# The second score matmul of each head on 64 array rows instead of 128, the two heads of a pair on different rows

## The chip, the cores and the metric

The kernel runs on one core of a Trainium2 chip. The metric is device time in microseconds of one execution, lower is better. The kernel before has a median of 1741.18 us over three runs (1739.69 to 1743.17).

## What is computed

One layer of a diffusion backbone over 1024 latent and 128 context tokens, in fp32 with D_MODEL 1024: a modulated RMSNorm, one input projection, a Fourier mixer beside windowed attention, gates, an output projection, and an MLP with 4096 hidden units. The change lies in the attention: 16 query heads in 4 groups that share a key and value head, head size 64, blocks of 128 queries. In the reference:

```python
scores = jnp.einsum('btkgd,blkd->bkgtl', qb, k_all,
                    preferred_element_type=jnp.float32) * (HEAD_DIM ** -0.5)
if mask is not None:
    scores = jnp.where(mask[None, None, None], scores, NEG_INF)
sink_col = ...
p = jax.nn.softmax(jnp.concatenate([scores, sink_col], axis=-1), axis=-1)[..., :-1]
return jnp.einsum('bkgtl,blkd->btkgd', p.astype(v_all.dtype), v_all)
```

A latent block sees up to 384 latent keys around it and the 128 cached ones (512 keys, 384 at the two ends); the context block sees 128 keys.

## The kernel before

**Two halves of a number.** TensorE (PE) multiplies in a rounded fp32 type. To keep fp32 accuracy a value is split into hi (rounded) and lo (the rest, `sub`, L138), and a product is made as hi·hi + hi·lo + lo·hi (`mm3`, L191 to L193). The scores use the short head size to do this in two matmuls instead of three. `qhl` holds, for each of four heads, 64 columns of q hi and then 64 columns of q lo; transposed (L670) and copied (L675) it is `qT`, with q hi in array rows 0 to 63 and q lo in rows 64 to 127. The keys lie twice, one copy above the other: `kth` has k hi in both halves, `ktl` has k lo in both. The first matmul (L691, `qT` with `kth`) gives q hi·k hi + q lo·k hi, the second (L692, `qT` with `ktl`) adds q hi·k lo + q lo·k lo, into the same PSUM tile `s`, of which there are two.

**Staging.** A unit is a group of four heads and a block of 128 queries: 4 groups by 9 blocks are 36 units. For each, `attention_q` projects q (24 matmuls of 256 columns, L191 to L193), rotates it on VectorE (DVE, `apply_rope`), splits and transposes it; `attention_scores` makes the scores pair by pair (two heads e = 0, 1 in each of two pairs): two matmuls a head, then on DVE the mask and the row maximum (L693), on ScalarE (ACT) the exponential (L705), on GpSimd (POOL) the division (L715). `attention_out` transposes the probabilities (L729), splits them (ACT L734, DVE L138) and multiplies with v (L739, L740) into `o`. There are 144 matmuls of L691 and 144 of L692: of each 96 with 512 columns, 32 with 384 and 16 with 128. Between the units stand gate projections (`mm`, 24 matmuls of 384 columns each), put there to fill PE.

**What sets the order.** The order on each engine is chosen by a scheduler when the kernel is built, from the dependences, the buffers and its own estimate of times. Each engine then runs its instructions in that fixed order, and waits where an operand or a buffer isn't ready. So the places of the score matmuls among the others can differ from the order in the source.

**Matmuls on fewer than 128 rows.** The kernel has few. Where the modulation is folded (`make_h`, L437) 14 small fp32 matmuls multiply 4 rows with 2 columns, and two multiply 2 rows; the built program gives these 32 of the array's rows, and shows them twice each in the trace, since fp32 takes two passes. Another fp32 matmul, L265, folds on all 128 rows and gives 16 columns.

Of the kernel before, what the change touches and what calls it, by code (L numbers as in the profile page):

```python
# [10 lines left out]
F32 = mybir.dt.float32  # L11
# [3 lines left out]
ALU = mybir.AluOpType  # L15
# [3 lines left out]
P = 128  # L19
# [38 lines left out]
def backbone_kernel(  # L58
# [25 lines left out]
    nc = tc.nc  # L84
    uid = [0]

    def nm(s):
        uid[0] += 1
        return f"{s}_{uid[0]}"
# [47 lines left out]
    def sub(eng, dst, raw, hi):  # L137
        eng.tensor_tensor(dst, raw, hi.bitcast(F32), ALU.subtract)  # L138
# [51 lines left out]
    def mm3(out, ah, al, bh, bl, start, stop):  # L190
        nc.tensor.matmul(out, ah, bh, start=start, stop=False)  # L191
        nc.tensor.matmul(out, ah, bl, start=False, stop=False)  # L192
        return nc.tensor.matmul(out, al, bh, start=False, stop=stop).ins  # L193
# [133 lines left out]
    with ExitStack() as sf:  # L327
# [169 lines left out]
        for o in range(0, NDFT, 1024):  # L497
            n = min(1024, NDFT - o)
# [8 lines left out]
        for gi in range(4):  # L507
# [17 lines left out]
            for s in range(4):  # L525
                r = slice(s * 512, (s + 1) * 512)
                anchor = mm3(pa, sth[:, s], stl[:, s], dhi[:, r], dlo[:, r], s == 0, s == 3)
            for s in range(2):
                r = slice(2048 + s * 256, 2304 + s * 256)
# [39 lines left out]
    with ExitStack() as s1x:  # L569
# [15 lines left out]
        def apply_rope(dst, src, t, hi=None):  # L585
            a = p1.tile([P, 4, HD], F32, tag="ra", name=nm("ra"), bufs=2)
            b = p1.tile([P, 4, HD], F32, tag="rb", name=nm("rb"), bufs=1)
            nc.vector.tensor_tensor(a, src, rope[:, 0, t, :].unsqueeze(1).to_broadcast([P, 4, HD]), ALU.mult)
            sw = src.rearrange("p h (d two) -> p h d two", two=2)
            sn = rope[:, 1, t, :].unsqueeze(1).to_broadcast([P, 4, HD])  # L590
            nc.vector.tensor_tensor(
                b.rearrange("p h (d two) -> p h d two", two=2),
                sw[:, :, :, ::-1],
                sn.rearrange("p h (d two) -> p h d two", two=2),
                ALU.mult,
            )
            nc.vector.tensor_tensor(dst, a, b, ALU.add)
            if hi is not None:
                nc.vector.tensor_tensor(hi, a, b, ALU.add)

        def put_v(src, t):
            vv = p1.tile([P, NG, 2, HD], F32R, tag="qhl", name=nm("qhl"), bufs=2)
# [35 lines left out]
        q1 = s1x.enter_context(tc.tile_pool(name="q1", bufs=1, space=PSUM))  # L638
# [14 lines left out]
        def attention_q(g, i, qw):  # L653
            psq = q1.tile([P, 512], F32, tag="q", name=nm("q"), bufs=1)
            r = slice(i * P, (i + 1) * P)
            for k in range(KC):
                wh, wl = qw[k // 4]
                mm3(psq[:, :256], h_hi[k][:, r], h_lo[k][:, r], wh[:, k % 4, :], wl[:, k % 4, :], k == 0, k == KC - 1)
            qsrc = psq[:, :256].rearrange("p (h d) -> p h d", h=4)
            qr = p1.tile([P, 4, HD], F32, tag="qr", name=nm("qr"), bufs=2)  # L660
            qhl = p1.tile([P, 4, 2, HD], F32R, tag="qhl", name=nm("qhl"), bufs=2)
            if i < 8:
                apply_rope(qr, qsrc, i, qhl[:, :, 0, :])
            else:
                nc.scalar.copy(qr, qsrc)
                nc.scalar.copy(qhl[:, :, 0, :], qsrc)
            sub(nc.vector, qhl[:, :, 1, :], qr, qhl[:, :, 0, :])
            psT = q1.tile([P, 512], F32R, tag="ptp", name=nm("ptp"), bufs=2)
            for h in range(4):
                ins = nc.tensor.transpose(  # L670
                    psT[:, h * P : (h + 1) * P], qhl[:, h].rearrange("p a d -> p (a d)"), identr
                )
            anchor = ins.ins
            qT = p1.tile([P, 4, P], F32R, tag="qT", name=nm("qT"), bufs=2)
            nc.scalar.copy(qT.rearrange("p h t -> p (h t)"), psT)  # L675
            return qT, anchor

        def attention_scores(g, i, qT):
            k0, nb = KWIN[i]
            n = nb * P  # L680
            m0 = MWIN[i] * P
            pts = []
            for pr in range(2):
                pt = p1.tile([P, 2, 516], F32, tag="pt", name=nm("pt"), bufs=4)
                mx = p1.tile([P, 8], F32, tag="mx", name=nm("mx"), bufs=4)
                h0 = g * 4 + pr * 2
                nc.gpsimd.tensor_copy(pt[:, :, n : n + 1], sink8[:, h0 : h0 + 2].unsqueeze(2))
                for e in range(2):
                    h = pr * 2 + e
                    sp = q1.tile([P, 512], F32, tag="s", name=nm("s"), bufs=2)  # L690
                    nc.tensor.matmul(sp[:, :n], qT[:, h, :], kth[:, k0 * P : k0 * P + n], start=True, stop=False)  # L691
                    nc.tensor.matmul(sp[:, :n], qT[:, h, :], ktl[:, k0 * P : k0 * P + n], start=False, stop=True)  # L692
                    nc.vector.tensor_tensor_reduce(  # L693
                        out=pt[:, e, :n],
                        in0=sp[:, :n],
                        in1=mask[:, m0 : m0 + n],
                        scale=1.0,
                        scalar=sink8[:, h0 + e : h0 + e + 1],
                        op0=ALU.add,
                        op1=ALU.max,  # L700
                        accum_out=mx[:, e : e + 1],
                    )
                nc.vector.tensor_scalar(mx[:, 2:4], mx[:, 0:2], -0.125, None, ALU.mult)  # L703
                for e in range(2):
                    nc.scalar.activation(  # L705
                        pt[:, e, : n + 1],
                        pt[:, e, : n + 1],
                        AF.Exp,
                        bias=mx[:, 2 + e : 3 + e],
                        scale=0.125,  # L710
                        accum_out=mx[:, 4 + e : 5 + e],
                    )
                nc.vector.reciprocal(mx[:, 6:8], mx[:, 4:6])  # L713
                for e in range(2):
                    nc.gpsimd.tensor_scalar(pt[:, e, :n], pt[:, e, :n], mx[:, 6 + e : 7 + e], 1.0, ALU.mult, ALU.mult)  # L715
                pts.append(pt)
            return pts
# [31 lines left out]
        kth = p1.tile([P, 12 * P], F32R, name="kth")  # L749
        ktl = p1.tile([P, 12 * P], F32R, name="ktl")  # L750
# [53 lines left out]
        for q in range(3):  # L804
            put_k(kv[0][0], q)
        nxt = attention_q(0, 0, qw)
        pending = None
        for s, (g, i) in enumerate(units):
            qT, anchor = nxt
            if s + 1 < len(units):  # L810
                g1, i1 = units[s + 1]
                if i1 == 0:
                    qw = load_q(g1)
                nxt = attention_q(g1, i1, qw)
                anchor = nxt[1]
            pts = attention_scores(g, i, qT)
            if i == 0 and g:
                put_k(kv[g][0], 2)
            if g + 1 < NG:
                if i == 2:  # L820
                    kv[g + 1] = load_kv(g + 1)
                if i == 4:
                    put_k(kv[g + 1][0], 0)
                if i == 7:
                    put_k(kv[g + 1][0], 1)
            if pending is not None:
                attention_out(*pending)
                if s % SKIP:
                    filler(1, anchor)
                if s <= 30:  # L830
                    mod_step(MOD_A)
            pending = (g, i, pts, kv[g][1])
            if s >= len(units) - 2:
                if s == len(units) - 2:
                    filler(100, anchor)
                    load_fx()
                f_unit(NF)
# [34 lines left out]
    with ExitStack() as sao:  # L872
# [11 lines left out]
        for m in range(KC):  # L884
            if m < 7:
                hi, lo = ER[:, 2 * m * NT : (2 * m + 1) * NT], ER[:, (2 * m + 1) * NT : (2 * m + 2) * NT]
            else:
                hi, lo = (p3.tile([P, NT], F32R, name=nm("at7")) for _ in range(2))
            for j in range(NJ):
                r = slice(j * CH, (j + 1) * CH)  # L890
# [930 lines left out]
```

## Time and profile before

| | us |
|---|---|
| median of three runs | 1741.18 |
| the profiled execution | 1740.25 |
| its span, first to last instruction | 1738.5 |
| attention stage (the units), from the span's start | about 276 to 722 |
| PE busy over the span | 1660.2 (95%) |
| DVE, ACT, POOL busy | 1217.1, 846.3, 229.2 |

Times in the trace are from the span's start. PE is TensorE's matmuls, PEld its weight loads (LDWEIGHTS), which run beside the matmul before. A matmul's row gives its start and a duration with the time it spends in the array's pipeline, so matmuls overlap: what one costs in a stream is the distance from its start to the next start. "128\*128 128x512" is array rows by columns, then the shape of what it writes or reads. "x4" stands for four that follow each other. The mean granted TensorE clock is 0.982 of full speed.

### The profile page before, as it was taken

To read this page: it belongs to the slowest core of one execution; us is meant where nothing else is said; L and a number is where in the kernel's file an instruction comes from. 1 tells how busy PE (TensorE), PEld (TensorE's weight loads), DVE (VectorE), ACT (ScalarE), POOL (GpSimd) and SP (SyncE) were. 2 spreads that over 40 slices of the span, in tenths; PEclk is the share of its full clock that TensorE was granted. 3 is DMA by queue.
4 is the path that set the end of the run, shared out by engine and by line. 5 is a ranking of instruction groups with operands and counts; after the bars stand their busy time and mean duration, and the time that the engine had idled before them with its cause. 6 is when DMAs were issued, how large, how long until landed. Compare 5 with 4: busy or idle time off the path is not lost.

```text
span 1738.5 us, 26472 instructions
## 1 busy us (share of the span) xinstructions
PE 1660.2 (95%) x9101; PEld 1480.9 (85%) x9101; DVE 1217.1 (70%) x2538; ACT 846.3 (49%) x1676; POOL 229.2 (13%) x310
## 2 busy tenths in 40 slices
PE   6999988999999999999899889999999999999998
PEld 5788878999899999999888688888888788888886
DVE  7595455686767777659968878767666488777764
ACT  7443134555646556655326663444444345444542
POOL 3410002212213222202211400000000100000000
PEclk9999999999999999999999989999999999999999
DMA  9462383032222211478655435444444997566751
GB/s 293 124 189 82 129 233 76 28 96 68 60 53 63 59 35 40 147 241 281 211 165 204 160 103 176 164 146 164 151 146 155 231 378 252 190 193 193 238 176 61
DMA packets 218759, 267.44 MB, mean 154 GB/s; under 512 B 30768, under 2 KB 150144, under 8 KB 218624
## 3 DMA queue, kind: packets, MB, share of 16 engines
q1 hardware_dynamic: 210368, 255.79, 46.3%
q0 software_dynamic: 8256, 9.96, 2.2%
q8 instruction: 72, 1.18, 0.3%
q14 instruction: 63, 0.52, 0.1%
HBM read 196.20 MB, written 69.48 MB: 153 GB/s over the span
## 4 chain that ended last, share of the span: by engine, by line
PE 43%; DVE 4%; DMA 2%; ACT 1%; issue 1%; POOL 0%; SPq 0%; ACTq 0%; DVEq 0%; POOLq 0%
PE x L1570 6%; PE x L1569 6%; PE x L1568 6%; PE x L1179 5%; PE x L1181 5%; PE x L1180 5%; PE x L1015 1%; PE x L1016 1%; PE x L1017 1%; DVE macc L302 1%; PE mm L1570 1%; PE mm L1569 1%; PE mm L1568 1%; PE mm L1226 1%; PE mm L1225 1%
## 5 line engine op out<-in xcount | busy, mean ns | idle before, releaser
L138 DVE TENSOR_TENSOR wlo<-wraw,whi 128x1024 fp32r<-128x1024 f32 x100 | 125.8, 1260 | 58.1 <-ACT whi L143 57.7
L143 ACT CAST whi<-wraw 128x1024 fp32r<-128x1024 f32 x98 | 102.5, 1049 | 88.8 <-DMA wraw<-in_w_ff_dram 21.0
L1569 PE MATMUL x<-BR 128*128 128x512 f32 x336 | 131.4, 391 | 0.0
L1570 PE MATMUL x<-BR 128*128 128x512 f32 x336 | 130.9, 391 | 0.0
L1568 PE MATMUL x<-BR 128*128 128x512 f32 x336 | 129.9, 391 | 0.0
L715 POOL TENSOR_SCALAR pt<-pt,mx 128x512 f32<-128x512 f32 (+2 forms) x144 | 99.1, 701 | 211.1 <-DVE mx L713 198.1
L705 ACT ACTIVATE pt<-pt,mx 128x513 f32<-128x513 f32 (+2 forms) x144 | 94.8, 661 | 55.8 <-DVE mx L703 55.1
L192 PE MATMUL mm<-BR,whi 128*128 128x384 f32 x336 | 113.8, 339 | 0.0
L693 DVE CUSTOM_DVE_ANT_0 pt<-s,mask,sink 128x512 f32<-128x512 f32 (+2 forms) x144 | 94.2, 673 | 22.2 <-PE ptp L729 15.0
L191 PE MATMUL mm<-BR,whi 128*128 128x384 f32 x304 | 105.3, 346 | 0.0
L193 PE MATMUL mm<-BR,wlo 128*128 128x384 f32 x304 | 102.9, 339 | 0.0
L1541 ACT CAST BR<-aa 128x512 fp32r<-128x512 f32 x80 | 49.7, 621 | 103.9 <-PE x L1569 49.1
L138 DVE TENSOR_TENSOR pl<-ptp,ph 128x512 fp32r<-128x512 f32 (+1 forms) x136 | 85.9, 640 | 15.6 <-ACT ph L734 14.5
L734 ACT CAST ph<-ptp 128x512 fp32r<-128x512 f32 (+1 forms) x136 | 72.7, 548 | 40.8 <-PE ptp L729 39.2
L302 DVE SCALAR_TENSOR_TENSOR macc<-mraw,siluc,macc 128x256 f32<-128x256 f32 x168 | 85.1, 544 | 10.5 <-DMA mraw<-in_w_ada_dram 10.3
L1179 PE MATMUL x<-BR,whi 128*128 128x512 f32 (+2 forms) x204 | 82.3, 403 | 6.2 <-ACT ZR L1203 3.3
L1181 PE MATMUL x<-BR,wlo 128*128 128x512 f32 (+2 forms) x204 | 81.1, 398 | 3.5 <-DVE wlo L138 3.5
L1180 PE MATMUL x<-BR,whi 128*128 128x512 f32 (+2 forms) x204 | 80.5, 395 | 0.0
L729 PE MATMUL ptp<-ident,pt 128*128 128x128 f32 x496 | 75.1, 273 | 3.0 <-ACT qT L675 3.0
L138 DVE TENSOR_TENSOR BR<-aa,BR 128x512 fp32r<-128x512 f32 x80 | 55.2, 689 | 32.0 <-ACT BR L1541 31.6
L1568 PEld LDWEIGHTS x<-BR 128*128 128x128 f32 x336 | 63.5, 189 | 13.2
L1569 PEld LDWEIGHTS x<-BR 128*128 128x128 f32 x336 | 63.4, 189 | 13.3
(422 smaller groups left out, 5119.6 us busy)
## 6 DMA issues: line engine op xcount, KB each, us to landing
aa<-hr_d SPq DMA_DIRECT2D x108, 256.0 KB, 3.4
ab<-in_w_ff_dram SPq DMA_DIRECT2D x108, 256.0 KB, 3.4
hr_d<-ZR SPq DMA_DIRECT2D x104, 256.0 KB, 4.1
wraw<-in_w_in_dram SPq DMA_DIRECT2D x40, 512.0 KB, 4.1
wraw<-in_w_ff_dram SPq DMA_DIRECT2D x34, 512.0 KB, 3.8
mraw<-in_w_ada_dram SPq DMA_DIRECT2D x96, 128.0 KB, 3.1
wraw<-in_w_out_dram SPq DMA_DIRECT2D x24, 512.0 KB, 3.8
z_d<-z SPq DMA_DIRECT2D x48, 192.0 KB, 1.9
```

Of the source, the lines that this page charges most:

```text
L138: eng.tensor_tensor(dst, raw, hi.bitcast(F32), ALU.subtract)
L143: nc.scalar.copy(hi, raw)
L191: nc.tensor.matmul(out, ah, bh, start=start, stop=False)
L192: nc.tensor.matmul(out, ah, bl, start=False, stop=False)
L193: return nc.tensor.matmul(out, al, bh, start=False, stop=stop).ins
L302: nc.vector.scalar_tensor_tensor(acc[:, tok, :], wa, sc_, acc[:, tok, :], ALU.mult, ALU.add)
L1179: nc.tensor.matmul(po, wh, xh, start=(k == 0 and not cont), stop=False, skip_group_check=cont)
L1180: nc.tensor.matmul(po, wh, xl, start=False, stop=False, skip_group_check=cont)
L1181: nc.tensor.matmul(po, wl, xh, start=False, stop=(k == 3), skip_group_check=cont)
L1568: nc.tensor.matmul(ps, xh, bh, start=start, stop=False, skip_group_check=cont)
L1569: nc.tensor.matmul(ps, xh, bl, start=False, stop=False, skip_group_check=cont)
L1570: nc.tensor.matmul(ps, xl, bh, start=False, stop=stop, skip_group_check=cont)
```

## The change

The second matmul of each head now runs on 64 array rows. For head e = 0 of a pair these are rows 0 to 63, for e = 1 rows 64 to 127. So that q hi lies in those rows, the odd heads have hi and lo exchanged in `qhl` (`q_hi` takes the places 0 and 3 of a pair's four, `q_lo` the places 1 and 2). The first matmul is not touched: it sums both halves, in either order. The second gives q hi·k lo alone; the term q lo·k lo is no longer computed. Both PSUM tiles of a pair are taken before the first of its matmuls, and in the source the four matmuls of a pair now stand as first, first, second, second, with the two 64-row ones side by side.

```diff
@@ apply_rope
             nc.vector.tensor_tensor(dst, a, b, ALU.add)
             if hi is not None:
-                nc.vector.tensor_tensor(hi, a, b, ALU.add)
+                a2, b2 = (x.rearrange("p (r e) d -> p r e d", r=2) for x in (a, b))
+                nc.vector.tensor_tensor(hi, a2, b2, ALU.add)
@@ attention_q
             qhl = p1.tile([P, 4, 2, HD], F32R, tag="qhl", name=nm("qhl"), bufs=2)
+            q4 = qhl.rearrange("p (r e) a d -> p r (e a) d", r=2)
+            q_hi, q_lo = q4[:, :, 0:4:3, :], q4[:, :, 1:3, :]
             if i < 8:
-                apply_rope(qr, qsrc, i, qhl[:, :, 0, :])
+                apply_rope(qr, qsrc, i, q_hi)
             else:
                 nc.scalar.copy(qr, qsrc)
-                nc.scalar.copy(qhl[:, :, 0, :], qsrc)
-            sub(nc.vector, qhl[:, :, 1, :], qr, qhl[:, :, 0, :])
+                nc.scalar.copy(q_hi, qsrc.rearrange("p (r e) d -> p r e d", r=2))
+            sub(nc.vector, q_lo, qr.rearrange("p (r e) d -> p r e d", r=2), q_hi)
@@ attention_scores
+                sps = [q1.tile([P, 512], F32, tag="s", name=nm("s"), bufs=2) for _ in range(2)]
+                kr_ = slice(k0 * P, k0 * P + n)
                 for e in range(2):
-                    h = pr * 2 + e
-                    sp = q1.tile([P, 512], F32, tag="s", name=nm("s"), bufs=2)
-                    nc.tensor.matmul(sp[:, :n], qT[:, h, :], kth[:, k0 * P : k0 * P + n], start=True, stop=False)
-                    nc.tensor.matmul(sp[:, :n], qT[:, h, :], ktl[:, k0 * P : k0 * P + n], start=False, stop=True)
+                    nc.tensor.matmul(sps[e][:, :n], qT[:, pr * 2 + e, :], kth[:, kr_], start=True, stop=False)
+                for e in range(2):
+                    half_ = slice(64 * e, 64 * e + 64)
+                    nc.tensor.matmul(sps[e][:, :n], qT[half_, pr * 2 + e, :], ktl[half_, kr_], start=False, stop=True)
+                for e in range(2):
+                    sp = sps[e]
                     nc.vector.tensor_tensor_reduce(
```

In the changed kernel the first matmul is L694, the second L697; the other lines of the attention move down by 3 to 7. The number of matmuls is the same (9061 in the built program). Since the scheduler sets the order, the pairs have to be looked for in the built program. PE's rows for the two pairs of one unit of the first group follow; `s` with its number is one head's scores, `o` the product with v, `q` a later unit's projection, `ptp` a transpose. The first pair, before:

```order
L729 MATMUL ptp_4848<-ident,pt_4631 128x128 x4
L691 MATMUL s_4963<-kth,qT_4811 128x512
L692 MATMUL s_4963<-ktl,qT_4811 128x512
L691 MATMUL s_4967<-kth,qT_4811 128x512
L692 MATMUL s_4967<-ktl,qT_4811 128x512
L739 MATMUL o_4706<-ph_4712,vg_2724 128x256
```

and in the changed program:

```order
L736 MATMUL ptp_4848<-ident,pt_4631 128x128 x4
L694 MATMUL s_4963<-kth,qT_4811 128x512
L694 MATMUL s_4964<-kth,qT_4811 128x512
L697 MATMUL s_4963<-ktl,qT_4811 128x512
L697 MATMUL s_4964<-ktl,qT_4811 128x512
L746 MATMUL o_4706<-ph_4712,vg_2724 128x256
```

The two first matmuls stand together now, and the two on 64 rows (L697) are neighbours, with a 128-row matmul ahead and one behind. The second pair of the same unit stands so on PE before:

```order
L193 MATMUL q_5296<-qwh_5292,BR 128x256
L691 MATMUL s_4980<-kth,qT_4811 128x512
L692 MATMUL s_4980<-ktl,qT_4811 128x512
L739 MATMUL o_4847<-ph_4853,vg_2724 128x256
L740 MATMUL o_4847<-pl_4854,vg_2724 128x256
L739 MATMUL o_4847<-ph_4853,vg_2724 128x256
L740 MATMUL o_4847<-pl_4854,vg_2724 128x256
L739 MATMUL o_4847<-ph_4866,vg_2724 128x256
L691 MATMUL s_4984<-kth,qT_4811 128x512
L692 MATMUL s_4984<-ktl,qT_4811 128x512
L740 MATMUL o_4847<-pl_4867,vg_2724 128x256
```

and in the changed program:

```order
L193 MATMUL q_5296<-qwh_5292,BR 128x256
L694 MATMUL s_4980<-kth,qT_4811 128x512
L697 MATMUL s_4980<-ktl,qT_4811 128x512
L746 MATMUL o_4847<-ph_4853,vg_2724 128x256
L747 MATMUL o_4847<-pl_4854,vg_2724 128x256
L746 MATMUL o_4847<-ph_4853,vg_2724 128x256
L747 MATMUL o_4847<-pl_4854,vg_2724 128x256
L746 MATMUL o_4847<-ph_4866,vg_2724 128x256
L694 MATMUL s_4981<-kth,qT_4811 128x512
L697 MATMUL s_4981<-ktl,qT_4811 128x512
L747 MATMUL o_4847<-pl_4867,vg_2724 128x256
```

Here nothing moved: each 64-row matmul stands alone between matmuls on 128 rows. Over the whole program the 144 matmuls of L697 form 31 neighbouring pairs (19 with 512 columns, 7 with 384, 5 with 128) and 82 that stand alone (58, 18 and 6). That makes 113 stretches on 64 rows, and 226 places where PE goes from 128 rows to 64 or back; the program before has none of these. At 17 of the 226 the neighbour on 128 rows is a transpose (L736, L673).

## The prediction

> **What bounds the kernel now.** First the shares of the page, then the attention stage by itself.
>
> ```profile
> PE 1660.2 (95%) x9101; PEld 1480.9 (85%) x9101; DVE 1217.1 (70%) x2538; ACT 846.3 (49%) x1676; POOL 229.2 (13%) x310
> ```
>
> The stretch of the units, from the view by windows (length; then busy time and count of PE, PEld, DVE, ACT, POOL; granted clock, DMA share, GB/s):
>
> ```profile
> 276.00:722.00 446.00, 432.18 (x3055) 418.33 (x3055) 323.99 (x925) 265.26 (x669) 113.01 (x212) 0.99 0.21 58
> ```
>
> The change touches only this stage. PE is busy for 432.2 of its 446.0 us at a granted clock of 0.99, and DVE for 324.0. So PE sets the stage. How much slack PE has shows in the list of its waits in the same stretch:
>
> ```profile
> engine line waited for: us in total, times, longest us
> PE o L740 <- DVE pl L138: 5.3, 7, 1.4
> PE ptp L729 <- ACT qT L675: 3.0, 2, 2.1
> PE ptp L670 <- DVE pl L138: 2.2, 3, 1.2
> PE ptp L670 <- DVE mx L703: 1.8, 1, 1.8
> ```
>
> These four sum to 12.3 us of 446, and no wait at L691 or L692 is among them. Whatever the score matmuls cost PE more or less, the end of the kernel gets nearly in full. Next, what a score matmul costs now, by groups of line and shape, and one pair in order of time (start, duration), matmuls and then weight loads:
>
> ```profile
> L692 PE MATMUL s<-ktl,qT 128*128 128x512 f32 x96 | 38.4, 400 | 0.0
> L692 PE MATMUL s<-ktl,qT 128*128 128x384 f32 x32 | 10.8, 339 | 0.0
> L692 PE MATMUL s<-ktl,qT 128*128 128x128 f32 x16 | 4.1, 275 | 0.0
> ```
>
> ```profile
> 553.15 0.39 PE L691 MATMUL s<-kth,qT 128*128 128x512 f32 x1
> 553.38 0.40 PE L692 MATMUL s<-ktl,qT 128*128 128x512 f32 x1
> 553.62 0.39 PE L691 MATMUL s<-kth,qT 128*128 128x512 f32 x1
> 553.85 0.39 PE L692 MATMUL s<-ktl,qT 128*128 128x512 f32 x1
> 554.08 0.28 PE L193 MATMUL q<-qwh,BT 128*128 128x256 f32 x1
> ```
>
> ```profile
> 553.15 0.19 PEld L692 LDWEIGHTS s<-ktl,qT 128*128 128x128 f32 x1
> 553.38 0.19 PEld L691 LDWEIGHTS s<-kth,qT 128*128 128x128 f32 x1
> ```
>
> The starts are 0.23 us apart though each row lasts 0.39: a stream of 512 columns costs 0.23 each. The weights of a matmul are loaded while the one before it runs (those of the 553.38 matmul from 553.15), so they cost nothing. With 384 columns a matmul costs 0.17, with 128 columns 0.11:
>
> ```profile
> 277.15 0.34 PE L692 MATMUL s<-ktl,qT 128*128 128x384 f32 x1
> 277.32 0.33 PE L691 MATMUL s<-kth,qT 128*128 128x384 f32 x1
> ...
> 719.78 0.27 PE L691 MATMUL s<-kth,qT 128*128 128x128 f32 x1
> 719.89 0.27 PE L692 MATMUL s<-ktl,qT 128*128 128x128 f32 x1
> ```
>
> The whole second pass is thus 96 × 0.23 + 32 × 0.17 + 16 × 0.11 = 29.3 us. Half of it is the most that pairing could ever save.
>
> **The change: the gain.** Only neighbours can run side by side. The built order has 31 neighbouring pairs, 19, 7 and 5 by width. If the second of each cost nothing, that would be 19 × 0.23 + 7 × 0.17 + 5 × 0.11 = 6.1 us. The 82 alone gain nothing, since a matmul's cost goes by its columns: the rows it uses do not appear in it. The lower bound of the gain is nothing. I take a value between: two weight loads that can't go ahead start about 0.11 us apart (L437 below, four in 0.52 with 0.19 for the last), so the second matmul starts 0.11 after the first and a pair saves 0.12, 0.06 or nothing: 19 × 0.12 + 7 × 0.06 = 2.7 us.
>
> **The change: the price of going from 128 rows to 64 and back.** The trace has no 64-row matmul. The nearest rows are the 4-row ones of L437, which the program puts on 32 of the array's rows. In order of time, PE and then PEld:
>
> ```profile
> 59.97 0.39 PE L230 MATMUL x<-wlo,BR 128*128 128x512 f32 x1
> 60.19 0.39 PE L231 MATMUL x<-whi,BR 128*128 128x512 f32 x1
> 60.51 0.60 PE L437 MATMUL mm<-pairsum,mr 4*128 4x2 f32 x4
> 61.04 0.39 PE L424 MATMUL mm<-whi,crep 128*128 128x256 f32 x1
> 61.27 0.28 PE L424 MATMUL mm<-wlo,crep 128*128 128x256 f32 x1
> 61.39 0.28 PE L424 MATMUL mm<-whi,crep 128*128 128x256 f32 x1
> ```
>
> ```profile
> 59.97 0.19 PEld L231 LDWEIGHTS x<-whi,BR 128*128 128x128 f32 x1
> 60.51 0.52 PEld L437 LDWEIGHTS mm<-pairsum,mr 4*128 4x128 f32 x4 [0.35 <-issue]
> 61.04 0.19 PEld L424 LDWEIGHTS mm<-whi,crep 128*128 128x128 f32 x1
> 61.15 0.19 PEld L424 LDWEIGHTS mm<-wlo,crep 128*128 128x128 f32 x1
> ```
>
> Two things happen here. From 60.19 to 60.51 are 0.32 us, where the stream gives 0.22 to 0.23: PE stands for 0.09 more before it starts on the other rows. And the weight load of L437 starts at 60.51, together with its matmul, and not at 60.19; the same at 61.04 on the way back. PEld's row says "issue" for this idle time: no engine was waited for. The first matmul behind such a place is therefore late by a weight load: L424 at 61.04 lasts 0.39 instead of 0.28 and the next starts 0.23 later instead of 0.12, 0.11 more. A change of rows so costs 0.09 + 0.11 = 0.20 us when the neighbours are long enough to have hidden the load, which those of 512, 384 and 256 columns are.
>
> Is it the rows, or the small fp32 matmul? L265 is the control, fp32 with 16 columns on all 128 rows, first PE and then PEld:
>
> ```profile
> 353.44 0.34 PE L193 MATMUL mm<-BT,wlo 128*128 128x384 f32 x1
> 353.62 0.29 PE L265 MATMUL mm<-red,quads 128*128 128x16 f32 x2
> 353.76 0.36 PE L740 MATMUL o<-pl,vg 128*128 128x256 f32 x1
> ```
>
> ```profile
> 353.45 0.36 PEld L265 LDWEIGHTS mm<-red,quads 128*128 128x128 f32 x2
> ```
>
> Its weights load from 353.45, ahead of its start at 353.62, which comes 0.18 after the one before, the plain distance for 384 columns. So nothing stands still on the way in, and it is the rows. [...]
>
> **The sum.** 226 changes × 0.20 = 45.2 us. At 17 of them the neighbour is a transpose, and next to transposes a load is partly unhidden already:
>
> ```profile
> 720.01 0.62 PE L729 MATMUL ptp<-ident,pt 128*128 128x128 f32 x4
> 720.38 0.42 PE L191 MATMUL mm<-BR,whi 128*128 128x384 f32 x1
> 720.64 0.34 PE L192 MATMUL mm<-BR,whi 128*128 128x384 f32 x1
> ```
>
> The 384 columns of 720.38 take 0.26 to the next start, not 0.17. So I take off 17 × 0.09 = 1.5. The pairs give back 2.7. PE's waits of 12.3 us can shrink, since PE is slower and the others are not; most of them are for operands made a few instructions before, so I take a quarter, 3. The work on DVE and ACT for `qhl` has the same element counts, cut into other pieces, and lies beside a PE that is the bound: nothing. Taking both `s` tiles before the first matmul of a pair makes the second head's first matmul wait until DVE's L693 has read both tiles; the order shows it delayed or moved where that matters, and PE showed no wait there, so nothing. No DMA moves. 45.2 − 1.5 − 2.7 − 3 = 38 us more. Against the profiled execution, 1740.25 us (span 1738.5 and 1.75 around it, 0.93 under the median), this gives 1778 us.
>
> Bounds for one change of rows: from below nothing, if 64 rows are chosen without standing still, since no 64-row row excludes it. From above PE waits until the row of a 512-column matmul ends, 0.39 after its start, which is 0.16 late, and loads for 0.11: 0.27 × 226 = 61 us, 1796 after the same deductions of some 5. I take 0.20 because L437 is the same kind of step, on fewer rows.
>
> **The rivals.**
>
> The first ends on the other side: **no standstill at 64 rows**, the pairs run side by side. For it: the only evidence against is on 32 rows, with fp32 operands. Against it: the control shows that the type isn't the cause. It gives 6.1 us less at best, 1734; it decides if a change costs under 6.1 / 226 = 0.027 us. [...]
>
> The second: **only the standstill, the load stays hidden**. With 64 rows in use, the other half of the array might take weights early. Against it: L424's load at 61.04 had 96 free rows and still waited. 226 × 0.09 = 20 us, less 6 for pairs and waits: 1755.
>
> The third: **nothing either way**, the rows are only an address: 1740. The pairs don't overlap, and changes cost nothing.
>
> The fourth: **more than forecast**. The standstill lasts to the end of the row (0.27 a change), or the pairs don't overlap and the new order adds waits: about 1795.
>
> **How the numbers follow.** Forecast 0.65, first rival 0.07, second 0.15, third 0.05, fourth 0.08. The predicted time is the forecast's, 1778. The range goes from 1750, under the second rival, to 1795: it holds the forecast nearly whole, most of the second rival and half of the fourth, about 8 in 10. A measurement of this kernel tells about 0.2% (3.5 us) from no change. Faster by more is the first rival, 0.07; within 0.2% the third, 0.05; slower by more is the rest, 0.88.
>
> **What would show it.** In the changed trace the distance from the L694 ahead of a single L697 to that L697 should be about 0.32 us with 512 columns instead of 0.23, and the weight load of L697 should start with its matmul. The same should be seen at the next 128-row matmul: a late load, a duration about 0.11 longer. Two neighbouring L697 should start about 0.11 apart, and not 0.23. The attention stage should be some 38 us longer and the others equal in length. The prediction is wrong if L697's weights load ahead as those of L692 do, if the standstill is much shorter or longer than 0.09, or if the time appears in another stage.

## The result

| | before | after |
|---|---|---|
| median of four runs, us | 1741.35 (1739.69 to 1743.17) | 1767.43 (1760.65 to 1770.18) |
| profiled execution | 1740.25 | 1769.16 |
| its span | 1738.5 | 1767.4 |

The changed kernel is slower: the ratio is 1.0144, 95% interval 1.0112 to 1.0176. The forecast was 1778 in a range of 1750 to 1795. By the traces the stage from the first score matmul to the last product with v goes from 466.4 to 498.4 us (4.2 us of that is one gate projection of 24 matmuls, which the scheduler now puts inside it and no longer behind it). Nothing else changed its length by more than 3 us.

The groups of the score matmuls after, by line and shape (a mean holds the array's pipeline too):

```profile
L697 PE MATMUL s<-ktl,qT 64*128 64x512 f32 x96 | 38.4, 500 | 0.0
L694 PE MATMUL s<-kth,qT 128*128 128x512 f32 x96 | 37.6, 425 | 0.0
L697 PE MATMUL s<-ktl,qT 64*128 64x384 f32 x32 | 11.0, 438 | 0.0
L697 PE MATMUL s<-ktl,qT 64*128 64x128 f32 x16 | 3.6, 324 | 0.0
```

"64\*128" says that the rows did change. A 512-column matmul of the second pass lasts 500 ns, where it lasted 400. Why shows in order of time, first PE, then PEld, in a stretch with a neighbouring pair (544.51) and two single ones (546.98 and 547.83):

```profile
543.79 0.33 PE L193 MATMUL mm<-BT,wlo 128*128 128x384 f32 x1
543.96 0.62 PE L694 MATMUL s<-kth,qT 128*128 128x512 f32 x2
544.51 0.50 PE L697 MATMUL s<-ktl,qT 64*128 64x512 f32 x2
544.94 0.39 PE L192 MATMUL q<-qwl,BT 128*128 128x256 f32 x1
545.17 0.28 PE L193 MATMUL q<-qwh,BR 128*128 128x256 f32 x1
...
546.98 0.49 PE L697 MATMUL s<-ktl,qT 64*128 64x512 f32 x1
547.40 0.50 PE L694 MATMUL s<-kth,qT 128*128 128x512 f32 x1
547.83 0.50 PE L697 MATMUL s<-ktl,qT 64*128 64x512 f32 x1
548.26 0.39 PE L191 MATMUL q<-qwh,BR 128*128 128x256 f32 x1
548.48 0.28 PE L192 MATMUL q<-qwl,BR 128*128 128x256 f32 x1
548.60 0.28 PE L193 MATMUL q<-qwh,BR 128*128 128x256 f32 x1
```

```profile
543.79 0.36 PEld L694 LDWEIGHTS s<-kth,qT 128*128 128x128 f32 x2
544.51 0.19 PEld L697 LDWEIGHTS s<-ktl,qT 64*128 64x128 f32 x2 [0.36 <-issue]
544.94 0.19 PEld L192 LDWEIGHTS q<-qwl,BT 128*128 128x128 f32 x1 [0.24 <-issue]
...
547.83 0.18 PEld L697 LDWEIGHTS s<-ktl,qT 64*128 64x128 f32 x1 [0.24 <-issue]
548.26 0.19 PEld L191 LDWEIGHTS q<-qwh,BR 128*128 128x128 f32 x1 [0.24 <-issue]
```

Three things are to be seen. The weights of each matmul behind a change of rows start with the matmul itself (547.83 in both lists; within 3 ns at 225 of the 226 changes, 30 ns at the other), those of the others go ahead, by 117 ns at the median of the stage. From 547.83 to 548.26 are 0.43 us for 512 columns, and then 0.22 for 256 columns, where 0.23 and 0.12 are plain. And the pair at 544.51 takes 0.50 and 0.43 to the next start, the same as the single one: its second matmul costs nothing. In the records the two start 3 to 4 ns apart, in all 31 pairs.

Added up over the stage (each start-to-start distance less the plain one of its width: 0.232, 0.174, 0.119, 0.109 us for 512, 384, 256, 128 columns), the 226 changes cost 44.0 us, 0.195 each. The pairs give 6.1 back. PE's three longest entries among its waits in the trace of after:

```profile
PE ptp L736 <- ACT qT L678: 2.1, 1, 2.1
PE o L747 <- DVE pl L138: 1.8, 4, 0.5
PE o L746 <- DVE at L753: 1.0, 1, 1.0
```

### The profile page after: what moved, and what is told of

It reads as the page before. It is cut to its first block, busy times and chain, and to the rows that moved or that the text cites. A ratio compares the mean times of both kernels' runs of the same rounds, so it can differ in the third digit from the quotient of the medians.

```text
span 1767.4 us, 26476 instructions
## 1 busy us (share of the span) xinstructions
PE 1692.9 (96%) x9101; PEld 1473.2 (83%) x9101; DVE 1223.6 (69%) x2538; ACT 845.4 (48%) x1676; POOL 224.4 (13%) x310
## 4 chain that ended last, share of the span: by engine, by line
PE 73%; DVE 9%; DMA 8%; issue 3%; ACT 2%; POOL 0%; SPq 0%; DVEq 0%; ACTq 0%; POOLq 0%
PE x L1577 6%; PE x L1575 6%; PE x L1576 6%; PE x L1186 5%; PE x L1188 5%; PE x L1187 5%; PE mm L191 4%; PE mm L192 3%; PE mm L193 3%; PE ptp L736 3%; DMA mraw<-in_w_ada_dram 3%; PE s L697 2%; PE q L191 2%; DVE macc L302 2%; PE q L192 2%
## 5 line engine op out<-in xcount | busy, mean ns | idle before, releaser
L138 DVE TENSOR_TENSOR wlo<-wraw,whi 128x1024 fp32r<-128x1024 f32 x100 | 126.7, 1268 | 62.0 <-ACT whi L143 61.5
L138 DVE TENSOR_TENSOR pl<-ptp,ph 128x512 fp32r<-128x512 f32 (+1 forms) x136 | 86.4, 640 | 28.4 <-ACT ph L741 27.4
L736 PE MATMUL ptp<-ident,pt 128*128 128x128 f32 x496 | 77.6, 274 | 2.9 <-ACT qT L678 2.1
L138 DVE TENSOR_TENSOR BR<-aa,BR 128x512 fp32r<-128x512 f32 x80 | 55.0, 687 | 31.7 <-ACT BR L1548 31.2
L1576 PEld LDWEIGHTS x<-BR 128*128 128x128 f32 x336 | 63.1, 188 | 13.1
```

The source lines that it names most:

```text
L736: nc.tensor.transpose(pst[:, bi, e, :], pt[:, e, b * P : (b + 1) * P], ident)
L1576: nc.tensor.matmul(ps, xh, bl, start=False, stop=False, skip_group_check=cont)
```

## The experiments

The theory: a change between 128 and 64 rows costs 0.195 us (a standstill of 0.095, and a weight load of 0.10 that cannot go ahead), and the second of a neighbouring pair is free. The rivals: the new order costs, not the rows; or a 64-row matmul is dear in itself. The numbers of changes could be varied without any other difference, because the scheduler makes the same order for 64 and for 128 rows.

**All rows again, in the new order.**

```diff
-                    half_ = slice(64 * e, 64 * e + 64)
+                    half_ = slice(0, P)
```

> The changed kernel with its second score matmul on all 128 rows again (one slice is different, so q lo times k lo is back); every engine's order is that of the changed kernel, instruction for instruction. Theory (each change between 128 and 64 rows costs 0.095 us of standstill and 0.10 us of unhidden weight load): no changes are left, so the time is that of the kernel before, 1741 within 4 us. Rival (the new order is what costs, since both score tiles are taken first): it stays near 1767.

Measured: 1737.73 us against 1740.08 for the kernel before in the same comparison, ratio 0.9982 (0.9971 to 0.9994). The order costs nothing, the rows cost all of it. The rival of the order falls.

**All 64-row matmuls alone, in the old order.**

```diff
                 for e in range(2):
+                    half_ = slice(64 * e, 64 * e + 64)
                     nc.tensor.matmul(sps[e][:, :n], qT[:, pr * 2 + e, :], kth[:, kr_], start=True, stop=False)
-                for e in range(2):
-                    half_ = slice(64 * e, 64 * e + 64)
                     nc.tensor.matmul(sps[e][:, :n], qT[half_, pr * 2 + e, :], ktl[half_, kr_], start=False, stop=True)
```

> Second score matmul on 64 rows (q lo times k lo is left out, as in the changed kernel), but in the order of the kernel before, instruction for instruction: all 144 stand alone, 288 changes of rows in place of 226 and no pair. Theory: 288 x 0.196 = 56 us, of which PE's shorter waits take back about a quarter, 10 to 15: 1782 to 1788. Rival (the order costs): 1741, as before. Second rival (a 64-row matmul is dear in itself, whatever stands beside it): near 1767, as in the changed kernel, since there are 144 in both.

Measured: 1789.06, ratio 1.0283 (1.0266 to 1.0299). That is 49 us over before, and 22 us more than the changed kernel for the same 144 matmuls on 64 rows. So they are not dear in themselves; it goes by the changes. The time is 1 us over the theory's interval.

**All pairs neighbours.**

```diff
                 for e in range(2):
-                    nc.tensor.matmul(sps[e][:, :n], qT[:, pr * 2 + e, :], kth[:, kr_], start=True, stop=False)
-                for e in range(2):
-                    half_ = slice(64 * e, 64 * e + 64)
-                    nc.tensor.matmul(sps[e][:, :n], qT[half_, pr * 2 + e, :], ktl[half_, kr_], start=False, stop=True)
+                    hi_mm = nc.tensor.matmul(sps[e][:, :n], qT[:, pr * 2 + e, :], kth[:, kr_], start=True, stop=False)
+                with tc.issue_after(hi_mm.ins):
+                    for e in range(2):
+                        half_ = slice(64 * e, 64 * e + 64)
+                        nc.tensor.matmul(sps[e][:, :n], qT[half_, pr * 2 + e, :], ktl[half_, kr_], start=False, stop=True)
```

> The changed kernel, with the two 64-row matmuls of a pair queued behind the pair's second 128-row one, so that 68 of 72 pairs are neighbours in the built order: 152 changes of rows. Theory: 152 x 0.196 = 29.8 us, less 13.9 for the second of each pair (44 x 0.232 + 16 x 0.174 + 8 x 0.109, if it starts with the first), less 3 to 8 of PE's waits: 1749 to 1754. Second rival (64 rows are dear in themselves): near 1767. If the pairs do not run side by side: 1763.

Measured: 1747.25, ratio 1.0038 (1.0019 to 1.0056). Better than the changed kernel by some 20 us, 2 us better than the theory's interval, and still slower than before: even with nearly every pair neighbouring, two changes cost 0.39 us and the pair saves 0.23 at most. (The interval was counted from the kernel before. On full rows this order is itself 5.7 us faster than that, as the run after the next shows; counted from there the theory gives 1743 to 1748, and the time lies inside.)

**The same pairs on the same rows.**

```diff
-            q_hi, q_lo = q4[:, :, 0:4:3, :], q4[:, :, 1:3, :]
+            q_hi, q_lo = q4[:, :, 0:4:2, :], q4[:, :, 1:4:2, :]
...
-                        half_ = slice(64 * e, 64 * e + 64)
+                        half_ = slice(0, 64)
```

> As the run with all pairs neighbours, in the same order, but q hi of all heads lies in rows 0 to 63, so both 64-row matmuls of a pair use the same rows and cannot run side by side; 152 changes of rows as there. Theory: 152 x 0.196 = 29.8 less 3 to 8 of waits: 1763 to 1768, which is 14 us over the run with different rows. Rival (the pairs gain nothing): the two runs are equal.

Measured: 1758.23, ratio 1.0118 (1.0090 to 1.0145), 11 us over the run with different rows. A pair in this trace, in order of time on PE, and then its weight loads on PEld:

```profile
541.86 0.73 PE L698 MATMUL s<-ktl,qT 64*128 64x512 f32 x2
542.52 0.39 PE L191 MATMUL q<-qwh,BR 128*128 128x256 f32 x1
542.75 0.28 PE L192 MATMUL q<-qwl,BR 128*128 128x256 f32 x1
```

```profile
541.86 0.29 PEld L698 LDWEIGHTS s<-ktl,qT 64*128 64x128 f32 x2 [0.37 <-issue]
```

The pair takes 0.66 us to the next start where the pair on different rows took 0.43: the difference is one 512-column stream. So it is the different rows that let two matmuls run at once. Over the stage the difference is 13.9 us by the distances, as expected; 3 of it are lost in longer waits of the faster run, which is why the medians differ by 11. The time is 5 us below the interval, which again was counted from the kernel before; counted from the same order on full rows it would be 1757 to 1762, and the time lies inside.

**The order of the neighbouring pairs, on all rows.** The edit is the one slice of the first experiment, made in the run with all pairs neighbours.

> The order of the run with all pairs neighbours, instruction for instruction, with the second matmul on all 128 rows (nothing is left out). It is that run's control. Theory: no changes of rows are left, so the run with all pairs should lie over it by its 152 changes less its 68 pairs, 15.2 us in its trace, less what PE's waits take back (5 to 8): this one at 1737 to 1742. Rival (the small loss of the run with all pairs came from its order): this one is at 1747 too.

Measured: 1735.11 against 1740.78, ratio 0.9974 (0.9962 to 0.9985), 2 us below the theory's interval. The control is faster than before, so the small loss of the run with all pairs is not its order's: the 152 changes and 68 pairs together cost 12 to 13 us. This kernel leaves no term out, and it is a quarter of a per cent faster than the kernel before. The first experiment's kernel, which leaves none out either, was 0.2% faster; the intervals of the two overlap.

The five and the two kernels together, each profiled execution; the costs are sums of distances over the plain ones, "long waits" those by more than 0.3 us; "median less before" is taken within each comparison, against the kernel before as measured there:

| | changes | their cost | pairs' gain | long waits | stage | median less before, us |
|---|---|---|---|---|---|---|
| before | 0 | | | 17.1 | 466.4 | |
| full rows, new order | 0 | | | 13.1 | 469.0 | -2.4 |
| pairs, full rows | 0 | | | 13.7 | 466.0 | -5.7 |
| pairs, different rows | 152 | 28.8 | 13.6 | 13.0 | 481.5 | +7.2 |
| pairs, same rows | 152 | 29.1 | 0 | 10.2 | 492.1 | +18.2 |
| the change | 226 | 44.0 | 6.1 | 8.9 | 498.4 | +26.1 |
| all alone | 288 | 55.5 | 0 | 11.1 | 511.7 | +49.0 |

All but the first and the last have the 4.2 us gate projection inside the stage. The price of a change lies between 0.189 and 0.195 us in all four.

**How much of PE's time reaches the end.** The forecast rested on PE setting the stage in both directions. The first test leaves the second pass out:

```diff
                 for e in range(2):
-                    nc.tensor.matmul(sps[e][:, :n], qT[:, pr * 2 + e, :], kth[:, kr_], start=True, stop=False)
-                for e in range(2):
-                    half_ = slice(64 * e, 64 * e + 64)
-                    nc.tensor.matmul(sps[e][:, :n], qT[half_, pr * 2 + e, :], ktl[half_, kr_], start=False, stop=True)
+                    nc.tensor.matmul(sps[e][:, :n], qT[:, pr * 2 + e, :], kth[:, kr_], start=True, stop=True)
```

> The second score matmul is left out for all heads (so q times k lo is missing), which takes 29.3 us of PE out of the stage at the distances in the trace. If PE sets the stage alone, 1741 falls by the full 29: 1712. The theory that PE's waits for the other engines grow when PE is faster and shrink when it is slower, as they did in the changed kernel (by 8 to 10 of 38), says that some of it is lost: 1718 to 1724.

Measured: 1738.99, ratio 0.9990 (0.9977 to 1.0002). Both expectations missed by far: 29 us of PE's work went, and nothing clear of the noise reached the end. PE's longest waits in its stage, and the whole stage by windows, first before and then in this run:

```profile
PE o L744 <- DVE pl L138: 7.8, 9, 1.5
PE ptp L673 <- DVE pl L138: 7.4, 5, 2.1
PE o L743 <- DVE at L750: 4.3, 6, 2.0
```

```profile
277.00:743.40 466.40, 452.58 (x3183) 438.66 (x3182) 329.23 (x937) 274.49 (x693) 113.73 (x214) 0.99 0.22 63
```

```profile
278.00:751.00 473.00, 443.36 (x3071) 425.86 (x3070) 327.16 (x940) 275.47 (x697) 112.37 (x214) 0.98 0.22 63
```

The stage is 471.8 us in this run, the 4.2 us of the gate projection included. Long waits grew from 17.1 to 38.7 us, the smaller excesses (up to 0.3 us over the plain distance each) by 9 more; 6 of these 9 are time at half the granted clock (last section). Is this a floor, or an unlucky order? Two more runs have other amounts of work and other orders, made from the run with the pairs on full rows:

```diff
-                        nc.tensor.matmul(sps[e][:, :n], qT[half_, pr * 2 + e, :], ktl[half_, kr_], start=False, stop=True)
+                        nc.tensor.matmul(sps[e][:, : n // 2], qT[half_, pr * 2 + e, :], ktl[half_, k0 * P : k0 * P + n // 2], start=False, stop=True)
```

> The second score matmul, on all 128 rows, runs over the first half of its columns only (the rest of q times k lo is missing). It takes about 13 us of PE out of the stage (a 256-column matmul costs 0.119, a 192-column one about 0.09). The scheduler makes an order of its own for it. If the stage has a floor that is not PE's work (what PE waits for DVE and ACT along each unit), as the run without the second matmul suggests: 1733 to 1740, as the runs with all the columns. If that run only had an unlucky order, and PE's work sets the stage: 1722 to 1728.

```diff
-                        nc.tensor.matmul(sps[e][:, :n], qT[half_, pr * 2 + e, :], ktl[half_, kr_], start=False, stop=True)
+                        nc.tensor.matmul(sps[e][:, :16], qT[half_, pr * 2 + e, :], ktl[half_, k0 * P : k0 * P + 16], start=False, stop=True)
```

> The second score matmul runs over its first 16 columns only (nearly all of q times k lo is missing). PE's work falls by some 25 us, nearly as in the run without the second matmul, but in another order of the scheduler. Floor: 1733 to 1742 again. Unlucky order there: well below, 1712 to 1728.

Measured: 1731.46 with half the columns (0.9932, 0.9913 to 0.9951) and 1741.42 with 16 (0.9998, 0.9987 to 1.0010). Half the second pass away, some 14 us of PE's work by the distances, brings 3.7 us against the same kernel with all of it. That is 1.5 us under what the floor expected (1733 to 1740) and 3.5 over what an unlucky order expected. Nearly all of it away, some 22 us, leaves it 6 us slower than with all of it, and where the kernel before is. The long waits are 18.5 and 28.5 us, where the same kernel with all of the second pass has 13.7. In all three orders most or all of the work that goes comes back, mainly as time in which PE waits or runs at half clock. That speaks for a limit near today's time, but it is argued from three orders: that no order could go below it is not shown. Which chain holds it there was not taken apart. PE's waits name DVE's L138 (the split of the probabilities) most, and in the run without the second pass L750 next.

The other direction, more work without any change of rows, again from the run with the pairs on full rows:

```diff
+                        nc.tensor.matmul(sps[e][:, :n], qT[half_, pr * 2 + e, :], ktl[half_, kr_], start=False, stop=False)
                         nc.tensor.matmul(sps[e][:, :n], qT[half_, pr * 2 + e, :], ktl[half_, kr_], start=False, stop=True)
```

> The second score matmul on all 128 rows is done twice (q times k lo is counted double), which adds 29.3 us of PE work to the stage and no change of rows. Theory: PE's added time reaches the end at the same rate as that of the changes of rows, 0.78 to 0.88 of it: 23 to 26 us over the run with the pairs in order on full rows, 1758 to 1762. If added work were hidden in PE's waits: 1735 to 1745.

Measured: 1754.03, ratio 1.0065 (1.0049 to 1.0081): 18.9 us over the same kernel with one second pass, less than the 23 to 26 expected. In the trace the long waits fall from 13.7 to 6.1 us, and what is left on PE's list is short:

```profile
PE ptp L738 <- ACT qT L678: 2.6, 2, 1.7
PE ptp L738 <- DVE ktl L138: 0.8, 1, 0.8
```

Smaller excesses included, PE's waits fell by 8.3 here (15.6 to 7.3), and by 8.5 in the changed kernel against the same order on full rows (18.6 to 10.1). But this is no fixed allowance, and no fixed rate either. By the stages of the table, each against its control on full rows, the waits took back 10 of 55.5 us in the run with all alone, 3 of 29 with the pairs on the same rows, and nothing of 15 with the pairs on different rows. (The last two traces also hold 3 us of half clock that their control's lacks.) Added work reached the end of the stage for the greater part in each of the five, in shares between 0.7 and 1.

## Why the prediction was right, and where its terms were off

**The mechanism** was right, and its price too: 43.7 us for the changes in the sum, 44.0 in the trace. The 4-row matmuls of L437, with L265 as their control, gave both halves of it: the standstill, 0.09 in the sum and 0.095 measured, and the load that can't go ahead, 0.11 and 0.10. That the total agrees within 1% is in part luck, since small misses of the two halves cancel. The rivals without a standstill, with the standstill alone, and with rows as a mere address (1734, 1755, 1740) are out: the step into L697 takes 0.327 us where 0.232 is plain, loads behind L697 start with their matmuls, and so do L697's own. The fourth is out too: the standstill does not last to the end of the row, which would have made the step 0.39.

**The pairs** were mis-sized: 2.7 us in the sum, 6.1 measured. The step that failed was to take the 0.11 us between the loads of L437, which follow each other on the same rows, for two loads on different rows. They run at once: the two loads at 544.51 take 0.19 us together, the two matmuls start 3 to 4 ns apart in all 31 pairs, and this pair takes 0.43 us to the next start. The run on the same rows, where a pair takes 0.66, shows that it takes the different rows.

**PE's waits** were mis-sized the other way: "a quarter, 3" of 12.3 us, measured 10.1 (8.2 in long waits). The prediction took the four longest entries of a list that holds 14.3 us in all; measured by the distances from start to start the waits of the kernel before are 20.1 us (17.1 in long ones), and half of them went. (The stretch 276 to 722 us, in which it read the list, ends behind the last score matmul; the last product with v starts at 743.3, and PE has no entry in between.) 1.6 of the 10.1 is the new order and 8.5 the slower PE. Together: 44.0 − 6.1 − 10.1 = 27.8 in the stage and 1.1 outside it (0.6 less ahead, 1.6 more behind, with the gate projection counted alike) make the 28.9 us between the profiled executions, where 38 were forecast.

**"Whatever the score matmuls cost PE more or less, the end of the kernel gets nearly in full"** was wrong in one of its two directions. More work arrived for the greater part: 0.7 to 1 of it by the stages, 18.9 of 29.3 us by the medians of the run with a doubled second pass. For less it does not hold: 29 us less work brought nothing. PE's small list of waits was read as slack, and the list says only how long PE waits at today's pace, not how near the next limit lies behind it. The first rival's gain of 6.1 us would hardly have arrived in full either: of 14 us less work 3.7 did.

**What would show it** was right on each point but the start of the second L697 and the size of the stage's growth: the entry took 0.327 us (median of 15 pairs and 0.3285 of 56 single ones, for 512 columns), the next 128-row matmul was 0.10 late (256 columns took 0.223 us to the next start, where 0.119 is plain), the stage grew by 28 us in place of 38, and the others didn't.

## What to carry to other kernels

Matmuls on part of the rows did not pay here in stretches of one or two: going in and out again cost 0.39 us, more than the 0.23 us that one neighbouring pair of 512 columns saves. Two such pairs in one stretch would save 0.46, an estimate from the same numbers that no run tested. Count the changes and the neighbours in the built order before the columns. The small matmuls that were already in the kernel priced the step well here (0.20 us in the sum, 0.195 measured), with a control to separate the cause. PE's busy share of 97% in the stage did not show whether less work on it brings anything: the run that left 29 us of it out did (1738.99 against 1740.78).

## What had not been expected of the hardware

Two 64-row matmuls on different rows share even their weight loads' time: both loads take 0.19 us from 544.51, where the single one's takes 0.18 from 547.83, and the pair takes the 0.43 us of a single one. On the same rows the second's load goes ahead as on 128 rows (0.66 for both, 0.43 and one stream of 0.23; the two loads take 0.29 together from 541.86, so the second ends before its matmul starts 0.34 behind the first), so in these traces only the change between 64 and 128 rows holds loads back, not the 64 rows as such.

Where PE waited more, its granted clock was lower: 0.95 against 1.00 at 63.54 and 67.86 us of busy time in 70. The same stretch on full rows and without the second pass, by windows:

```profile
350.00:420.00 70.00, 67.86 (x493) 65.79 (x492) 56.52 (x169) 37.90 (x102) 16.69 (x34) 1.00 0.32 85
```

```profile
350.00:420.00 70.00, 63.54 (x441) 61.57 (x440) 52.99 (x154) 36.71 (x97) 15.71 (x30) 0.95 0.29 81
```

The 0.95 is a mean. In its stage the second trace has the full clock but for single stretches of 3.4 us at one half. One of them by windows, then PE's rows in it and just behind it:

```profile
371.00:374.40 3.40, 3.09 (x13) 3.10 (x14) 3.40 (x11) 1.37 (x4) 0.00 (x0) 0.50 0.11 30
```

```profile
371.31 0.58 PE L744 MATMUL o<-pl,vg 128*128 128x256 f32 x1 [0.82 <-DVE pl L138]
...
373.24 0.52 PE L192 MATMUL mm<-BR,whi 128*128 128x384 f32 x1
373.56 0.52 PE L193 MATMUL mm<-BR,wlo 128*128 128x384 f32 x1
373.88 0.52 PE L191 MATMUL mm<-BR,whi 128*128 128x384 f32 x1
...
374.67 0.33 PE L191 MATMUL mm<-BR,whi 128*128 128x384 f32 x1
374.84 0.33 PE L192 MATMUL mm<-BR,whi 128*128 128x384 f32 x1
```

At half clock 384 columns take 0.32 us to the next start, at full clock 0.17. The stage without the second pass has six such stretches, which cost PE 8.9 us by the distances; the stage before has two (2.8 us), the ones on full rows in pairs and with the doubled second pass have none. In each of the six, PE had been idle for 1.64 to 2.51 of the 3.41 us just before; no other 3.41 us of that stage, counted in the same steps, has more than 1.42. With 16 columns the same count is less clean: one step with 1.61 us of idle time has no half clock behind it, and one with 1.43 has. That the waits bring the half clock fits these traces, and no run tested it by itself. If so, a wait can cost more than itself: of the 29 us of work that went, 22 came back as long waits and 6 as time at half clock. The granted clock of the whole program, averaged over all runs of each kernel, points the same way: 0.980 without the second pass, 0.982 before, 0.985 with it doubled.
